# Forming the weight sums of the vs projection by chained adding transfers, and reordering its token tiles, splits and late additions

## The chip, the cores and the metric

The kernel runs on one core of one Trainium2 chip. The metric is the device time of one execution in microseconds (us); lower is better. A core has TensorE (PE; its weight loads are PEld), VectorE (DVE), ScalarE (ACT), GpSimd (POOL) and SyncE (SP), each with an instruction queue of its own that is worked off in order, and 16 DMA engines that SP, ACT and POOL start transfers on.

## The reference

One layer of a streaming encoder for 1024 tokens and 1024 channels, in float32:

```python
h = rmsnorm(x, norm_g)
q, k, v, za, u, vs, zs, gm = split(h @ w_in)
a = window_sink_attention(rope(q), rope(k), v, sinks)
a = (a * silu(za)) @ w_att_out
sgo = chunked_spatial_gating(gelu(u), gelu(vs), sg_w, sg_b, ln_g, ln_b)
sgo = (sgo * silu(zs)) @ w_sg_out
ga, gs = split(sigmoid(gm + b_merge))
x = x + (ga * a + gs * sgo) @ w_o
out = rmsnorm(x, final_g)
```

The change lies in the first stage: the norm of x and the projection `vs`, whose gelu goes through a layer norm (hence statistics per token) into the spatial gating.

## The kernel before, in words

Every 1024 x 1024 x 1024 product is done by seven products of halves instead of eight (Strassen's scheme in Winograd's form). For `vs` the four quarters of the weights are a11, a12, a21, a22, and the sums are s1 = a21 + a22, s2 = s1 + a11, s3 = a11 + a21, s4 = a12 + s2; the tokens' forms are called b11, b21, t1, b22, t2, t3, t4. Every float32 operand is split in two: ACT casts a high part to the matmul's type (`nc.scalar.copy`, L155 in `split`, L557 in `form_of`), and DVE subtracts it to leave a low part (L156 and L558). Each product is then made of three, high by high, high by low and low by high. A product for one token tile of 128 tokens is 12 matmuls of 128x512.

The weights come packed in 128 x 1024 pieces; a quarter is two of them (c = 0 and 1). The sums of weights are made by transfers: `add_on(dst, src)` is a GpSimd DMA that adds its source to the destination in SBUF (L531). a11 lies in the slot T_t3h, a12 in T_t3l, s1 (loaded as a21, then a22 added) in T_t4h; the slots are taken by token forms later. Before the change a12 first takes a11 from DRAM and then s1, which makes s4, and a11 takes s1, which makes s2: eight adding transfers of 512 KB.

The tokens come in eight tiles. `first_tile(t)`, t = 0 to 3, and `second_tile(t)`, t = 4 to 7, load x (three buffers `wr` for all loads, L487), square it on ACT (L536) for the norm, compute the scale on DVE and ACT (L133 to L145), scale by it and by the gain on DVE (L544), transpose on PE (L548) into a bank `ps_sc`, and form b11 and b21, or t1 and b22. The gain lies in two PSUM banks for tiles 0 and 1 (`g_in`, made by a product with ones); before the change ACT copies these to SBUF (`g_sb`, L709) for the later tiles. `second_tile` also keeps what t2, t3 and t4 are made of: it makes the raw sum (L580, and a second addition, L586), a copy f22 of the second half (L585), and two adding transfers for t3 and t4.

Around the tiles stand the products: `first_product(t)` (b11 by a11 into `accs[t]`, b21 by a12, whose sum is x11: ACT copies, L668, DVE adds, L669), `by_s1(t)` (t1 by s1, into `t5s[t]`, which ACT copies negated, L674) and `by_s4(t)` (b22 by s4, onto the same bank). Then three calls of `late_product` run t2 by s2, t3 by s3 and t4 by a22, each over c and t, with gelus (`gelu_of`, L761) and statistics (L757) of finished quarters and the splits of what comes next beside the matmuls. The products for `u` begin after that (L341, in `gemm_pair`).

`part_of_early` issues, at certain places, one step of a list of 76 GpSimd transfers that form weight sums of later projections in DRAM (L296); a step waits for the matmul at which it was issued. With an argument n it issues at every n-th call; the list must be empty after the attention, where each hook calls it with 2.

The order of instructions on each engine is not the order of the source. A scheduler lays it down ahead of time from a cost model and priorities by source order: an instruction that the model has ready earlier may be put ahead of one that stands before it in the source. `after(second, first)` adds an order between two instructions of one engine without a wait. A helper example:

```python
def gelu_of(t, half=0):
    two = xh[:, t : t + 2, half_of(half)]
    after(nc.scalar.activation(two, two, AF.Gelu), last_cast)
```

Other small pieces that the text speaks of: the mixing weights `mix_w` are loaded into the buffer `wT`, which the squares use as scratch until tile 7, and a part is cleared by DVE (L767, L768); the sinks are loaded into `sink_sb` and negated on DVE into `nsink_sb` (L831, L834), which the attention reads much later.

Of the kernel before, what the change touches and what calls it, by code (L numbers as in the profile page):

```python
# [24 lines left out]
F32 = mybir.dt.float32  # L25
# [27 lines left out]
def hybrid_tile(  # L53
# [474 lines left out]
    casts = []  # L528
# [22 lines left out]
    def form_of(name, t, src, minus=False):  # L551
        hi, lo = (v[:, :, tokens(t)] for v in hb[name])
        if minus:
            casts.append(nc.scalar.mul(hi, src, -1.0))
            nc.vector.scalar_tensor_tensor(lo, src, -1.0, hi.bitcast(F32), op0=ALU.mult, op1=ALU.subtract)
        else:
            casts.append(nc.scalar.copy(hi, src))  # L557
            nc.vector.tensor_sub(lo, src, hi.bitcast(F32))  # L558
# [15 lines left out]
    def second_tile(t):  # L574
        xt, r = scale_of(t)
        if t == 4:
            hb.update(new_b(("t1", "b22")))
            f22.append(slot("t4l", dt=F32))
        pt = turned_half(xt, r, 0)
        nc.vector.tensor_sub(raw_sum(t), raw_sum(t), pt[:])  # L580
        nc.scalar.mul(nf12[t - 4][:], pt[:], -1.0)
        form_of("t1", t, by_k(raw_sum(t)))
        pt = turned_half(xt, r, 1)
        form_of("b22", t, by_k(pt[:]))
        nc.scalar.copy(f22[0][:, t - 4, :], pt[:])  # L585
        nc.vector.tensor_add(raw_sum(t), raw_sum(t), pt[:])  # L586
        add_on(nf12[t - 4][:], f22[0][:, t - 4, :])
        add_on(raw_b21(t), raw_sum(t))
# [29 lines left out]
    def split_w(name, c, src=None):  # L618
        hi, lo = pair_of_w()
        split(hi[:], lo[:], flat(two_k(raws[name], c)) if src is None else src)  # L620
        keep_w(name, c, hi, lo)
# [41 lines left out]
    def first_product(t):  # L663
        accs[t] = bank("mm" if t < 2 else "tp")
        vs_product(accs[t], "b11", t, "a11", True)
        m2 = bank("o")
        vs_product(m2, "b21", t, "a12", True)
        nc.scalar.copy(x_place(0, 0, t), m2[:])  # L668
        nc.vector.tensor_add(x_place(0, 0, t), x_place(0, 0, t), accs[t][:])  # L669
# [23 lines left out]
    x_in[2] = load_x(2)  # L693
    load_part("s1", "t4h", 1, 0)
# [6 lines left out]
    for c in range(2):  # L701
        add_on(flat(two_k(raws["a12"], c)), w_vs(0, 0, c))
    for c in range(2):
        add_on(flat(two_k(raws["a12"], c)), flat(two_k(raws["s1"], c)))
    raws["s4"] = raws["a12"]
    first_tile(1, second)
    g_sb = xh[:, 6:8, HALF:D]
    for half in range(2):
        after(nc.scalar.copy(g_sb[:, half, :], g_in[half][:]), casts[-1])  # L709
# [5 lines left out]
    second_tile(4)  # L715
    s1_hl = slot("t2h"), slot("t2l")
    for c in range(2):
        hi, lo = (two_k(v, c) for v in s1_hl)
        split(hi, lo, two_k(raws["s1"], c))
        for k in range(2):  # L720
            vs_w["s1", 2 * c + k] = hi[:, k, :], lo[:, k, :]
    first_product(2)
    second_tile(5)
    for c in range(2):
        add_on(flat(two_k(raws["a11"], c)), flat(two_k(raws["s1"], c)))
    raws["s2"] = raws["a11"]
    first_product(3)
    for c in range(2):
        split_w("s4", c)
    second_tile(6)  # L730
    by_s1(0)
# [4 lines left out]
    second_tile(7)  # L736
    by_s4(0)
# [7 lines left out]
    last_cast = casts[-1]  # L745
    split_w("s2", 0)
    hb.update(new_b(("t2",)))
    for t in range(4):
        form_of("t2", t, by_k(raw_sum(t)), True)
    by_s4(2)  # L750
# [21 lines left out]
    def late_product(name, weight, done, aside):  # L772
        for c in range(2):
            for t in range(4):
                pace[0] = vs_product(accs[t], name, t, weight, False, cs=(c,))
                if t % 3:
                    part_of_early(1)
                elif c:
                    part_of_early()
# [46 lines left out]
    split_w("a22", 1, a22[1][:])  # L826
    begin_job()
# [6 lines left out]
    nc.vector.tensor_scalar_mul(nsink_sb[:], sink_sb[:], -1.0)  # L834
# [1027 lines left out]
```

## Time and profile before

| | |
|---|---|
| time, median of 3 runs | 940.05 us (937.19 to 940.18) |
| the profiled execution | 941.21 us, span 939.4 us |
| PE busy | 904.0 us, 96% of the span |
| DVE, ACT, POOL busy | 697.7, 528.3 and 142.9 us |
| DMA moved | 210.10 MB, mean 224 GB/s |

The profile is one execution. Its rows read: line of the source, engine, operation, output<-inputs, shape, count, busy time, and the idle time of the engine just before with what ended it. In a timeline the first two numbers are the start and the time in us. A row of windows gives busy time of each engine in one stretch, the clock granted to TensorE as a share of full speed, the busy share of the DMA engines and the GB/s that they moved.

### The profile page before, as it was taken

Reading aid. Unit: us, or ns where it says so; the run is one execution under the profiler, and the core shown is the slowest. Engines: PE = TensorE matmul, PEld = TensorE weight load, DVE = VectorE, ACT = ScalarE, POOL = GpSimd, SP = SyncE. Lnnn points to the kernel's source line nnn. Section 1 sums busy time; section 2 is a strip of 40 time slices with the busy share of each in tenths; the row PEclk is TensorE's granted clock in tenths of the full one; section 3 lists DMA queues with packets and bytes.
Section 4 is the critical chain, followed back from the end, with each engine's and each line's share of the span. In section 5 each row is a group of like instructions: output and inputs, shape, how many; then the busy total and the mean of one; then the engine's idle time right before and its main releaser. Section 6 shows DMA issues by size and latency. Waiting matters only on the chain.

```text
span 939.4 us, 13191 instructions
## 1 busy us (share of the span) xinstructions
PE 904.0 (96%) x4284; PEld 749.5 (80%) x4284; DVE 697.7 (74%) x1263; ACT 528.3 (56%) x1060; POOL 142.9 (15%) x206
## 2 busy tenths in 40 slices
PE   8779989999999989999999999999998999999996
PEld 6557868888888878888888888888886887888885
DVE  6566866666667667888888888746799489669986
ACT  6547442333445357766766766746575466458443
POOL 2121222221202001011111111101100010210012
PEclk9798999999999999999999999999999999999999
DMA  8894987886877765777877669789878754999623
GB/s 283 192 242 100 233 249 178 173 174 168 287 241 245 268 197 166 185 199 206 215 199 265 225 172 254 213 273 376 277 240 315 266 191 152 291 298 311 206 104 121
DMA packets 131615, 210.10 MB, mean 224 GB/s; under 512 B 12666, under 2 KB 61050, under 8 KB 131547
## 3 DMA queue, kind: packets, MB, share of 16 engines
q1 hardware_dynamic: 109800, 149.21, 47.6%
q0 software_dynamic: 21600, 59.78, 28.1%
q8 instruction: 34, 0.56, 0.3%
q14 instruction: 35, 0.28, 0.1%
q10 hardware_dynamic: 146, 0.27, 0.1%
HBM read 148.27 MB, written 86.11 MB: 250 GB/s over the span
## 4 chain that ended last, share of the span: by engine, by line
PE 80%; DVE 8%; DMA 7%; issue 2%; ACT 1%; SPq 0%; DVEq 0%; ACTq 0%
PE ps_mm L341 35%; PE ps_o L341 25%; PE ps_sc L1192 3%; DMA wr<-in_w_dram 3%; PE ps_tp L341 3%; PE ps_o L1277 2%; PE ps_sc L341 2%; PE ps_tp L1236 2%; PE ps_sc L650 1%; DVE wl L156 1%; DMA sink_sb<-in_sinks_dram 1%; PE ps_tp L650 1%; PE ps_tp L880 1%; PE ps_mm L650 1%; DMA wT<-in_sg_w_dram 1%
## 5 line engine op out<-in xcount | busy, mean ns | idle before, releaser
L155 ACT CAST wh<-s 128x1024 fp32r<-128x1024 f32 (+1 forms) x78 | 78.2, 1004 | 88.9 <-PE ps_mm L341 49.7
L156 DVE TENSOR_TENSOR wl<-wr,wh 128x1024 fp32r<-128x1024 f32 (+1 forms) x78 | 73.3, 942 | 45.5 <-ACT wh L155 43.8
L155 ACT CAST wh<-wr 128x1024 fp32r<-128x1024 f32 (+1 forms) x78 | 64.1, 824 | 63.0 <-PE ps_mm L341 30.4
L156 DVE TENSOR_TENSOR wl<-s,wh 128x1024 fp32r<-128x1024 f32 (+1 forms) x78 | 91.5, 1173 | 9.2 <-ACT wh L155 8.6
L341 PE MATMUL ps_o<-T_t1h,wh 128*128 128x512 f32 x148 | 58.8, 397 | 0.8 <-ACT wh L155 0.7
L341 PE MATMUL ps_o<-T_b22h,wh 128*128 128x512 f32 x148 | 58.2, 393 | 0.0
L341 PE MATMUL ps_mm<-T_b11h,wl 128*128 128x512 f32 x140 | 55.2, 394 | 2.9 <-DVE wl L156 2.9
L341 PE MATMUL ps_o<-T_b22l,wh 128*128 128x512 f32 x148 | 57.8, 391 | 0.0
L341 PE MATMUL ps_o<-T_b22h,wl 128*128 128x512 f32 x148 | 57.8, 390 | 0.0
L341 PE MATMUL ps_o<-T_t1h,wl 128*128 128x512 f32 x148 | 57.7, 390 | 0.0
L341 PE MATMUL ps_o<-T_t1l,wh 128*128 128x512 f32 x148 | 57.6, 389 | 0.0
L341 PE MATMUL ps_mm<-T_t3h,wh 128*128 128x512 f32 x140 | 55.1, 393 | 2.3 <-ACT x L366 2.3
L341 PE MATMUL ps_mm<-T_t4h,wh 128*128 128x512 f32 x140 | 55.4, 396 | 0.6 <-DVE x L376 0.6
L341 PE MATMUL ps_mm<-T_b11h,wh 128*128 128x512 f32 x140 | 55.4, 396 | 0.0
L341 PE MATMUL ps_mm<-T_t3l,wh 128*128 128x512 f32 x140 | 54.6, 390 | 0.6 <-DVE T_t3l L156 0.6
L341 PE MATMUL ps_mm<-T_t2l,wh 128*128 128x512 f32 x140 | 55.2, 394 | 0.0
L341 PE MATMUL ps_mm<-T_b11l,wh 128*128 128x512 f32 x140 | 55.1, 394 | 0.0
L341 PE MATMUL ps_mm<-T_t2h,wl 128*128 128x512 f32 x140 | 55.0, 393 | 0.0
L341 PE MATMUL ps_mm<-T_t2h,wh 128*128 128x512 f32 x140 | 55.0, 393 | 0.0
L341 PE MATMUL ps_mm<-T_t4h,wl 128*128 128x512 f32 x140 | 54.8, 392 | 0.0
L341 PE MATMUL ps_mm<-T_t4l,wh 128*128 128x512 f32 x140 | 54.8, 391 | 0.0
L1205 ACT ACTIVATE pr<-ps_sc,sm 128x192 f32<-128x192 f32 (+2 forms) x128 | 50.9, 410 | 6.7 <-DVE sm L1201 5.8
(382 smaller groups left out, 2413.8 us busy)
## 6 DMA issues: line engine op xcount, KB each, us to landing
wr<-in_w_dram SPq DMA_DIRECT2D x86, 256.0 KB
sums<-in_w_dram POOLq DMA_DIRECT2D x20, 512.0 KB, 8.5
s<-sums SPq DMA_DIRECT2D x20, 512.0 KB
q_hl<-qhl SPq DMA_DIRECT2D x16, 512.0 KB
q<-q_hl SPq DMA_DIRECT2D x64, 128.0 KB
y_dr<-x POOLq DMA_DIRECT2D x28, 256.0 KB, 6.4
wr<-in_w_dram SPq DMA_DIRECT2D x12, 512.0 KB
g<-in_w_dram POOLq DMA_DIRECT2D x12, 512.0 KB, 6.9
```

Of the source, the lines that this page charges most:

```text
L155: nc.scalar.copy(hi, src)
L156: return nc.vector.tensor_sub(lo, src, hi.bitcast(F32))
L341: nc.tensor.matmul(acc, lt, rt, start=fresh and k == 0 and n == 0, stop=k == 3 and n == 2, skip_group_check=True,)
L650: mm = nc.tensor.matmul(acc[:], lt, rt, start=fresh and k == 0 and n == 0, stop=k == 3 and n == 2, skip_group_check=True,)
L880: nc.tensor.matmul(pm[:, t * P : (t + 1) * P], xh[:, half * 4 + t, g * P : (g + 1) * P], bias[-1][1][:, g % 4, :], start=True, stop=True,)
L1192: nc.tensor.matmul(sc[:, i, k0:], q_of[:, c, i * P : (i + 1) * P], kt[:, f, k0:], start=f == 0, stop=f == 1,)
L1205: nc.scalar.activation(held_in[c, i], sc[:, i, lo:hi], AF.Exp, bias=nmax[:, c, i : i + 1], scale=-1.0, accum_out=sums[:, c, i : i + 1],)
L1236: nc.tensor.transpose(dst, pr[:, i, block * P : block * P + width], ident[:])
L1277: nc.tensor.matmul(po[:, cs], lt, rt, start=n == 0, stop=n == len(terms) - 1)
```

## The change

- The weight sums are chained: s1 is added to a11 (s2) and that to a12 (s4). Six adding transfers instead of eight, all issued early; the two of a11 had stood after `second_tile(5)`.
- The gain for tiles 2 to 7 is loaded by a broadcasting DMA on SP's queue, ahead of the loads for s1, in place of two ACT copies.
- `split_behind` is a split whose two instructions are ordered behind the last cast and the last low part of the token tiles so far. It is used for s1 (now ahead of `second_tile(4)` in the source), s4 and the first piece of s2.
- The second raw addition and the transfer behind it leave `second_tile` for `raw_t2(t)`, which reads f22 from SBUF; it is called for tile 4 after tile 6, and for the others after tile 7. The additions to x11 leave `first_product` for `to_x11(t)`, ordered behind the low parts of tile 7.
- `last_cast`, behind which the gelus are ordered, is now the last cast of t2.
- The steps of `part_of_early` in the three late products are 4, 4, 4 and one more between the second and the third, instead of 5, 5 and 5.
- The negation of the sinks is ordered behind the last low part (that of t4).

```diff
--- before.py
+++ after.py
@@ -525,7 +525,7 @@
         return x_place(1, 0, t)
 
     g_of = list(g_in)
-    casts = []
+    casts, lows = [], []
 
     def add_on(dst, src):
         nc.gpsimd.dma_start(dst, src, accum_op=ALU.add)
@@ -552,10 +552,16 @@
         hi, lo = (v[:, :, tokens(t)] for v in hb[name])
         if minus:
             casts.append(nc.scalar.mul(hi, src, -1.0))
-            nc.vector.scalar_tensor_tensor(lo, src, -1.0, hi.bitcast(F32), op0=ALU.mult, op1=ALU.subtract)
+            lows.append(
+                nc.vector.scalar_tensor_tensor(lo, src, -1.0, hi.bitcast(F32), op0=ALU.mult, op1=ALU.subtract)
+            )
         else:
             casts.append(nc.scalar.copy(hi, src))
-            nc.vector.tensor_sub(lo, src, hi.bitcast(F32))
+            lows.append(nc.vector.tensor_sub(lo, src, hi.bitcast(F32)))
+
+    def split_behind(hi, lo, src):
+        after(nc.scalar.copy(hi, src), casts[-1])
+        after(nc.vector.tensor_sub(lo, src, hi.bitcast(F32)), lows[-1])
 
     def first_tile(t, scale=None):
         xt, r = scale or scale_of(t)
@@ -583,8 +589,10 @@
         pt = turned_half(xt, r, 1)
         form_of("b22", t, by_k(pt[:]))
         nc.scalar.copy(f22[0][:, t - 4, :], pt[:])
-        nc.vector.tensor_add(raw_sum(t), raw_sum(t), pt[:])
         add_on(nf12[t - 4][:], f22[0][:, t - 4, :])
+
+    def raw_t2(t):
+        nc.vector.tensor_add(raw_sum(t), raw_sum(t), f22[0][:, t - 4, :])
         add_on(raw_b21(t), raw_sum(t))
 
     def w_vs(i, j, c):
@@ -615,9 +623,9 @@
         for k in range(2):
             vs_w[name, 2 * c + k] = hi[:, half_of(k)], lo[:, half_of(k)]
 
-    def split_w(name, c, src=None):
+    def split_w(name, c, src=None, behind=False):
         hi, lo = pair_of_w()
-        split(hi[:], lo[:], flat(two_k(raws[name], c)) if src is None else src)
+        (split_behind if behind else split)(hi[:], lo[:], flat(two_k(raws[name], c)) if src is None else src)
         keep_w(name, c, hi, lo)
 
     def split_vs(c):
@@ -666,7 +674,9 @@
         m2 = bank("o")
         vs_product(m2, "b21", t, "a12", True)
         nc.scalar.copy(x_place(0, 0, t), m2[:])
-        nc.vector.tensor_add(x_place(0, 0, t), x_place(0, 0, t), accs[t][:])
+
+    def to_x11(t):
+        after(nc.vector.tensor_add(x_place(0, 0, t), x_place(0, 0, t), accs[t][:]), lows[-1])
 
     def by_s1(t):
         t5s[t] = bank("o" if t < 2 else "sc")
@@ -691,6 +701,8 @@
     for c in (2, 3):
         load_vs(c)
     x_in[2] = load_x(2)
+    g_sb = xh[:, 6:8, HALF:D]
+    nc.sync.dma_start(g_sb, norm_g.partition_broadcast(P).rearrange("p (h n) -> p h n", h=2))
     load_part("s1", "t4h", 1, 0)
     for c in (2, 3):
         split_vs(c)
@@ -699,41 +711,40 @@
     for c in range(2):
         add_on(flat(two_k(raws["s1"], c)), w_vs(1, 1, c))
     for c in range(2):
-        add_on(flat(two_k(raws["a12"], c)), w_vs(0, 0, c))
+        add_on(flat(two_k(raws["a11"], c)), flat(two_k(raws["s1"], c)))
     for c in range(2):
-        add_on(flat(two_k(raws["a12"], c)), flat(two_k(raws["s1"], c)))
-    raws["s4"] = raws["a12"]
+        add_on(flat(two_k(raws["a12"], c)), flat(two_k(raws["a11"], c)))
+    raws["s2"], raws["s4"] = raws["a11"], raws["a12"]
     first_tile(1, second)
-    g_sb = xh[:, 6:8, HALF:D]
-    for half in range(2):
-        after(nc.scalar.copy(g_sb[:, half, :], g_in[half][:]), casts[-1])
     g_of[:] = [g_sb[:, half, :] for half in range(2)]
     first_tile(2)
     first_product(0)
     first_tile(3)
     first_product(1)
-    second_tile(4)
     s1_hl = slot("t2h"), slot("t2l")
     for c in range(2):
         hi, lo = (two_k(v, c) for v in s1_hl)
-        split(hi, lo, two_k(raws["s1"], c))
+        split_behind(hi, lo, two_k(raws["s1"], c))
         for k in range(2):
             vs_w["s1", 2 * c + k] = hi[:, k, :], lo[:, k, :]
+    second_tile(4)
     first_product(2)
     second_tile(5)
-    for c in range(2):
-        add_on(flat(two_k(raws["a11"], c)), flat(two_k(raws["s1"], c)))
-    raws["s2"] = raws["a11"]
     first_product(3)
     for c in range(2):
-        split_w("s4", c)
+        split_w("s4", c, behind=True)
     second_tile(6)
+    raw_t2(4)
     by_s1(0)
     by_s1(1)
     load_part("s3", "t4h", 1, 0)
     for c in range(2):
         add_on(flat(two_k(raws["s3"], c)), w_vs(0, 0, c))
     second_tile(7)
+    for t in range(4):
+        to_x11(t)
+    for t in (5, 6, 7):
+        raw_t2(t)
     by_s4(0)
     by_s4(1)
     a22 = []
@@ -742,11 +753,11 @@
         nc.sync.dma_start(a22[c][:], w_vs(1, 1, c))
     by_s1(2)
     by_s1(3)
-    last_cast = casts[-1]
-    split_w("s2", 0)
+    split_w("s2", 0, behind=True)
     hb.update(new_b(("t2",)))
     for t in range(4):
         form_of("t2", t, by_k(raw_sum(t)), True)
+    last_cast = casts[-1]
     by_s4(2)
     by_s4(3)
     split_w("s2", 1)
@@ -773,10 +784,8 @@
         for c in range(2):
             for t in range(4):
                 pace[0] = vs_product(accs[t], name, t, weight, False, cs=(c,))
-                if t % 3:
+                if t % 2:
                     part_of_early(1)
-                elif c:
-                    part_of_early()
                 if c:
                     done(t)
                 if aside:
@@ -824,6 +833,7 @@
         for n, part in enumerate((wh, wl)):
             nc.tensor.matmul(row_sums[half][:], ones[:], part[:, half_of(half)], start=n == 0, stop=n == 1)
     split_w("a22", 1, a22[1][:])
+    part_of_early(1)
     begin_job()
     late_product("t4", "a22", to_x21, [split_next, lambda: gelu_of(4, 1), lambda: gelu_of(6, 1)])
     of_head = sinks.rearrange("(c e r) -> e c r", e=2, r=2)
@@ -831,7 +841,7 @@
         nc.sync.dma_start(
             sink_sb[e * 64 : (e + 1) * 64].rearrange("p (c r) -> p c r", r=2), of_head[e].partition_broadcast(64)
         )
-    nc.vector.tensor_scalar_mul(nsink_sb[:], sink_sb[:], -1.0)
+    after(nc.vector.tensor_scalar_mul(nsink_sb[:], sink_sb[:], -1.0), lows[-1])
     nc.sync.dma_start(bm_sb[:], b_merge)
     nc.sync.dma_start(lg_sb[:], ln_g)
     nc.sync.dma_start(lb_sb[:], ln_b)
```

## The prediction

> **What bounds the kernel now.** I read the page first, then windows, then the waits of PE, then the timelines of ACT and DVE around its long waits.
>
> ```profile
> span 939.4 us, 13191 instructions
> PE 904.0 (96%) x4284; PEld 749.5 (80%) x4284; DVE 697.7 (74%) x1263; ACT 528.3 (56%) x1060; POOL 142.9 (15%) x206
> ```
> ```profile
> 2.00:15.00 13.00, 12.50 (x34) 7.66 (x35) 7.58 (x18) 9.53 (x18) 2.16 (x2) 1.00 0.99 388
> 36.00:42.00 6.00, 6.00 (x27) 4.87 (x26) 3.43 (x11) 2.45 (x7) 0.00 (x0) 0.78 1.01 201
> 28.00:40.00 12.00, 8.54 (x27) 6.36 (x27) 6.15 (x13) 6.19 (x11) 3.46 (x4) 0.57 1.05 236
> 66.00:78.00 12.00, 9.22 (x29) 7.21 (x30) 6.77 (x13) 6.27 (x9) 3.45 (x4) 0.58 0.78 155
> 0.00:118.30 118.30, 101.30 (x412) 78.16 (x413) 79.19 (x154) 67.66 (x112) 27.15 (x40) 0.91 0.82 211
> 118.30:939.40 821.10, 802.69 (x3873) 671.32 (x3871) 618.47 (x1110) 460.62 (x948) 115.78 (x166) 0.99 0.75 225
> ```
>
> Columns of a window: its length, busy time of PE, PEld, DVE, ACT and POOL, granted clock, DMA share, GB/s. PE is the bound: 904.0 of 939.4 us. Idle time is uneven: 17.0 of 118.3 us before 118.3 us, at clock 0.91; 18.4 of 821.1 after it, at 0.99. The first U product starts at 118.30, so the first stretch is exactly the stage of the vs products, which the change rewrites:
>
> ```profile
> 118.30 0.39 PE L341 MATMUL ps_mm<-T_b11h,wh 128*128 128x512 f32 x1
> ```
>
> Its PE waits (total, times, longest):
>
> ```profile
> PE ps_tp L650 <- ACT T_b11h L557: 5.0, 1, 5.0
> PE ps_sc L548 <- DVE wr L544: 4.3, 1, 4.3
> PE ps_o L650 <- ACT xh L674: 2.1, 2, 1.8
> PE ps_tp L650 <- DVE T_b11l L558: 1.7, 1, 1.7
> PE ps_sc L650 <- ACT x L581: 1.2, 1, 1.2
> ```
>
> None of these is a slow instruction. Each is an engine standing, in its own order, before an instruction whose transfer has not landed, with ready work behind it:
>
> ```profile
> 28.15 1.04 ACT L155 CAST T_t2h<-T_t4h 128x1024 fp32r<-128x1024 f32 x1 [6.56 <-DMA T_t4h<-in_w_dram]
> 29.10 0.58 ACT L557 CAST T_b11h<-ps_sc 128x512 fp32r<-128x512 f32 x1
> 51.15 1.06 ACT L536 ACTIVATE wT<-wr 128x1024 f32<-128x1024 f32 x1 [2.08 <-DMA wr<-in_x_dram]
> 52.21 0.58 ACT L674 ACTIVATE xh<-ps_o 128x512 f32<-128x512 f32 x1
> ```
> ```profile
> 31.55 0.20 DVE L834 TENSOR_SCALAR nsink_sb<-sink_sb 128x8 f32<-128x8 f32 x1 [9.77 <-DMA sink_sb<-in_sinks_dram]
> 64.83 0.48 DVE L768 MEMSET wT<- 64x512 f32 x1 [5.15 <-DMA wT<-in_sg_w_dram]
> ```
>
> ACT holds the split of the weight sum s1 (reading T_t4h) ahead of tile 2's cast T_b11h and stands 6.56 us for the adding transfer: PE loses 5.0. DVE holds the sinks' negation, 9.77 us: tile 2's T_b11l is late and PE loses 1.7 more. The loss of 1.8 comes from x tile 6, for which ACT waits ahead of L674. The 4.3 us loss is DVE at the memset of the mixing weights. After each of the two long stops the clock is near half: 0.57 over 28 to 40 us, 0.58 over 66 to 78.
>
> **Part by part.** Sums are made against the profiled execution, 941.21 us (span 939.4 plus 1.8); the median shown, 940.05, is 1.2 below it.
>
> *s1's split behind tile 3's casts and low parts.* ACT's instruction after tile 2's transposes becomes T_b11h, and DVE's T_b11l, if the nsink step is moved too (it is: it stands behind the last low part, t4's). PE's 5.0 and 1.7 go: -6.7. The split now queues in front of token tile 4, and s1 is first read by by_s1(0). Its two casts of 1.04 and two low parts of about 1.23 lie beside the 24 matmuls of first_product(3), where PE is busy. ACT and DVE must then keep up:
>
> ```profile
> L156 DVE TENSOR_TENSOR wl<-T_t3h,wh 128x1024 fp32r<-128x1024 f32 x3 | 3.7, 1226 | 2.2 <-ACT wh L155 2.2
> ```
> ```profile
> 22.20:60.00 37.80, 29.12 (x127) 22.59 (x126) 23.70 (x52) 21.40 (x40) 7.85 (x10) 0.86 0.93 215
> ```
>
> In these 37.8 us, 25.6 after the gain summed below, ACT has 21.4 us of work and DVE 23.7, of which five additions of 0.68 move away. Both fit, ACT at 84%; this is why I count no gain beyond the stops named.
>
> *The half-speed stretch after it.* In 28 to 40 us PE was busy 8.54 us at 0.57; at full clock the same work takes 4.9: -3.7. It goes because its cause, the long stop, goes. The Trainium skill, "TensorE: Matmul & The Clock Gate", Part 1, has the clock halve after an idle window of about 3.4 us and return after about 3.4 us of sustained work. By that length the stretch is worth only an estimated 1.7 and the whole sum is 2.0 smaller; the row shows a longer one, and the row is used.
>
> *Tile 6's load.* In SP's queue it stands behind s3's load, which needs T_t4h free:
>
> ```profile
> SPq L604 <- DMA T_t3h<-T_t4h: 19.3, 2, 16.8
> ```
> ```profile
> 44.77 0.33 SPq L604 DMA_DIRECT2D T_t4h<-in_w_dram  x1
> 45.20 0.80 SPq L487 DMA_DIRECT2D wr<-in_x_dram  x1
> ```
>
> T_t4h is read last by the add that makes s2 (T_t3h), which was the eighth and last add in the queue and becomes the fourth of six. By the rates below it lands near 30.5 (16.4 + 4 x 2.6 + 2.7, and 1 for handing over). So x6 is issued near 31 us, not 45.2, and the 1.8 goes: -1.8. If the two loads change places the result is the same, since x6's buffer is free when tile 3 is transposed.
>
> *One add less per half, in a chain.* Before, a12 took a11 from DRAM and then s1; now s1 goes to a11 (s2) and s2 goes to a12 (s4). Adds fall from eight to six, but s4 hangs from three in a row instead of two.
>
> ```profile
> T_t3l<-in_w_dram POOLq DMA_DIRECT2D x2, 512.0 KB, 7.8
> T_t4h<-in_w_dram POOLq DMA_DIRECT2D x2, 512.0 KB, 12.6
> T_t3l<-T_t4h POOLq DMA_DIRECT2D x2, 512.0 KB, 9.7
> T_t3h<-T_t4h POOLq DMA_DIRECT2D x2, 512.0 KB, 11.7
> ```
> ```profile
> 14.31 1.04 POOL L531 DMA_DIRECT2D T_t3l<-in_w_dram  x1 [5.76 <-DVE st L140]
> 16.55 2.05 POOL L531 DMA_DIRECT2D T_t4h<-in_w_dram  x2
> 31.20 0.85 POOL L531 DMA_DIRECT2D T_t3l<-T_t4h  x1 [0.77 <-DMA T_t4h<-in_w_dram]
> ```
>
> The last number of the first four rows is the median time to landing. With the DMA full, plain loads moved 388 GB/s (2 to 15 us) and adds alone 201 (36 to 42): 1.35 and 2.6 us for 512 KB. The a12 adds at 14.31 stood ahead of s1's at 16.55; now s1's are first. Loads end near 16.4 (15 plus 1.35 for the gain's broadcast). Six adds and x4 and x5 are 15.7 + 2.7 = 18.4 us of transfers; with 2 us for handing over between links, an estimate by these rates puts the last half of s4 at about 37, where before its add was issued at 31.20 and landed about 9.7 later, near 41. s4 is first read at
>
> ```profile
> 52.84 0.74 PE L650 MATMUL ps_o<-wh,T_b22h 128*128 128x512 f32 x2 [1.81 <-ACT xh L674]
> ```
>
> which becomes 52.8 - 12.2 = 40.6; less 2.3 for cast and low part, it is wanted by 38.3. I take 0, with one or two us to spare; this is the thinnest cover of all, and the rivals price it.
>
> *Gain by broadcast instead of two ACT copies.*
> ```profile
> 18.48 0.61 ACT L709 COPY xh<-ps_tp 128x512 f32<-128x512 f32 x1
> 20.25 1.42 DVE L544 SCALAR_TENSOR_TENSOR wr<-wr,st,xh 128x512 f32<-128x512 f32 x2
> 24.13 0.61 PE L650 MATMUL ps_o<-s,T_b21l 128*128 128x512 f32 x2
> ```
>
> The two copies removed (0.61 each, from 18.48) ran while PE was busy until 24.7: 0. The added load stands in SP's queue ahead of s1's parts and x3. Like a load it costs 1.35 us of DMA; at double price, 2.7, x3 lands near 18, and its tile is scaled only after tile 2's. Tile 2's scaling, at 20.25, finds the gain landed near 13: 0 directly; its delay is in the 37 above.
>
> *Adds to x11 and raw sums, gelus, later.* Eight DVE additions like these move behind tile 7's low parts, and four statistics behind t2's:
>
> ```profile
> L586 DVE TENSOR_TENSOR xh<-xh,ps_sc 128x512 f32<-128x512 f32 x4 | 2.7, 684 | 0.1
> L757 DVE BATCH_NORM_STATS2 bn<-xh 128x6 f32<-128x512 f32 x14 | 8.9, 680 | 3.5 <-ACT xh L761 3.5
> ```
> ```profile
> 72.00:84.70 12.70, 12.70 (x48) 10.25 (x48) 6.50 (x11) 9.57 (x15) 1.71 (x2) 0.84 0.38 84
> 84.70:118.30 33.60, 33.60 (x149) 27.78 (x148) 29.04 (x48) 17.81 (x23) 9.11 (x14) 1.00 0.78 203
> ```
>
> At most 8 x 0.68 = 5.5 us enter the first of these stretches and 4 x 0.68 = 2.7 leave it: DVE 6.5 + 2.8 = 9.3 of 12.7. The second gets 2.7: 31.8 of 33.6. Both fit, the second tightly: 0, at most +2. The later adds of raw_b21 land after the last of these additions, and keep_t5, which overwrites their source, may stand on ACT for it: 0 to +2, covered by the t2 product, a third of that second stretch.
>
> *Early sums.* 13 steps instead of 15 are issued in this stage, and two more fall to the attention, whose 70 hooks at every second one take 35. No wait of PE there names them: 0, between -0.5 and +1.
>
> *Left as it is.* The memset at 64.83 has no new order, so I keep its 4.3, the 1.2 behind it and its slow clock (9.22 x 0.42 = 3.9).
>
> Sum: -6.7 - 3.7 - 1.8 = -12.2. 941.2 - 12.2 = 929.0 for the profiled execution; less 1.2, about 927 to 928 for the median. After 118.3 PE idles 2% only, so the gain is carried to the end. I forecast 927.
>
> **Rivals.**
>
> *The memset's stop goes too.* x6 and x7 load ten us earlier, so sg_w, issued behind tile 7's square, does too; if PE then still has by_s4 and by_s1 products in hand, the 4.3 + 1.2 + 3.9 = 9.4 also go: 927.8 - 9.4 = 918. For it: DVE is lightened. Against: its place in DVE's order still precedes tile 7's scaling.
>
> *s4 a few us late.* If its second half lands at about 42 to 43, ACT stands before the cast and by_s4 waits some 4 to 5 us: 932 to 933, and with a half-speed stretch after it 936.
>
> *Slower: the chain of three sets the pace.* Say each link takes what the slowest kind took, 12.6: issued near 15.5, s4 would land at 15.5 + 37.8 = 53.3, be split at 55.6, and PE, at 40.6, would stand 15.0 us and then lose 3.7 to the clock: 18.7 against 12.2, so 946. It decides from a landing near 46.8 (46.8 + 2.3 - 40.6 + 3.7 = 12.2). For it: landings of 9.7 to 12.6. Against: those had four adds in flight, and there are only two at a time in a chain. The Trainium skill, "DMA: Bandwidth & Descriptors", Anatomy of one DMA, gives a fixed 2.0 us plus bytes over 436 GB/s. By it a link is an estimated 3.2 us, and the rival is out of reach; the rows here, slower at every add, do not agree, and I keep the rival.
>
> *It does not carry.* The U weights and their sums, loaded behind a full DMA, could hold the U pairs at the old time: about 940. Against: they are issued by buffers that PE's progress frees, not by time.
>
> **How the numbers follow.** Forecast 0.45; memset also gone 0.20; s4 a few us late 0.20; not carried 0.06; slower 0.09. A measurement of this kernel can tell about 0.3%, 2.8 us. The first three are faster: 0.85; same 0.06; slower 0.09. The range runs from 916 (memset gone, with two us more) to 937 (s4 late, with slow clock), leaving out the last two cases and a little below.
>
> **What would show it.** Right: no ACT wait on T_t4h ahead of T_b11h, PE without a gap at 24.7, clock 1.00 over 28 to 40, the first L341 matmul near 106. The waits list should have no nsink_sb and no long L604 on T_t3h. Wrong: a PE wait at by_s4 with ACT's cast of T_t3l held by a transfer (the chain), a PE wait behind a new DVE or ACT stop of over 3 us, or an early first L341 matmul with new idle time between 118 and 160.

## The result and the profile after

The changed kernel takes 930.88 us (median of 4 runs, 930.13 to 932.78) against 939.87 us before on the same chip (4 runs, 937.19 to 940.18): a ratio of 0.9914 [0.989, 0.9937], 9.0 us less. The profiled execution takes 930.13 us against the 941.21 of the one before.

From the page of the kernel after, the span and the engines' busy time:

```profile
span 928.4 us, 13190 instructions
PE 898.3 (97%) x4284; PEld 746.8 (80%) x4284; DVE 697.0 (75%) x1263; ACT 526.9 (57%) x1058; POOL 141.5 (15%) x204
```

The same windows of it (length, busy PE, PEld, DVE, ACT, POOL, granted clock, DMA share, GB/s), the first two cut at its first U product:

```profile
0.00:107.93 107.93, 95.91 (x412) 75.00 (x413) 78.25 (x150) 66.40 (x110) 24.29 (x36) 0.98 0.81 222
107.93:928.40 820.47, 802.35 (x3873) 671.77 (x3871) 618.76 (x1114) 460.51 (x948) 117.18 (x168) 0.99 0.76 226
28.00:40.00 12.00, 8.93 (x43) 6.81 (x41) 7.62 (x17) 8.22 (x17) 2.06 (x3) 1.00 0.95 230
60.00:66.00 6.00, 5.92 (x23) 4.44 (x23) 4.80 (x9) 3.03 (x5) 0.86 (x1) 0.72 1.05 234
66.00:78.00 12.00, 12.00 (x55) 9.94 (x54) 6.58 (x9) 9.46 (x15) 1.31 (x2) 1.00 0.21 37
0.00:60.00 60.00, 48.06 (x207) 35.85 (x208) 39.08 (x88) 36.98 (x69) 14.52 (x22) 1.00 0.92 263
60.00:80.00 20.00, 19.92 (x84) 16.06 (x84) 13.38 (x20) 14.49 (x23) 2.48 (x3) 0.91 0.48 109
```

The whole gain lies in the stage of the vs products: it ends at 107.93 instead of 118.30, 10.4 us earlier, and the rest takes 820.5 instead of 821.1. Of the 10.4, 5.4 are PE work done at a better clock (busy 95.91 instead of 101.30) and 5.0 are idle time (12.0 instead of 17.0).

PE's waits of the stage (total, times, longest):

```profile
PE ps_sc L548 <- issue: 5.2, 2, 4.6
PE ps_sc L548 <- ACT T_t4l L591: 2.9, 1, 2.9
PE ps_sc L497 <- DVE T_b22l L493: 1.9, 1, 1.9
PE ps_sc L548 <- DVE wr L544: 1.6, 1, 1.6
```

The timelines of ACT, DVE, PE and SP's queue around the places that the prediction names (start, us, what it is, idle time before it and its releaser):

```profile
21.75 0.59 ACT L559 CAST T_b11h<-ps_sc 128x512 fp32r<-128x512 f32 x1 [0.55 <-PE ps_sc L548]
29.32 1.06 ACT L563 CAST T_t2h<-T_t4h 128x1024 fp32r<-128x1024 f32 x1
35.99 1.06 ACT L536 ACTIVATE wT<-wr 128x1024 f32<-128x1024 f32 x1 [3.70 <-DMA wr<-in_x_dram]
46.75 1.06 ACT L563 CAST wh<-T_t3l 128x1024 fp32r<-128x1024 f32 x1 [0.45 <-DMA T_t3l<-T_t3h]
48.20 1.05 ACT L536 ACTIVATE wT<-wr 128x1024 f32<-128x1024 f32 x1
57.36 0.48 DVE L779 MEMSET wT<- 64x512 f32 x1 [4.79 <-DMA wT<-in_sg_w_dram]
59.00 1.42 DVE L544 SCALAR_TENSOR_TENSOR wr<-wr,st,xh 128x512 f32<-128x512 f32 x2
49.69 0.62 PE L658 MATMUL ps_o<-wh,T_b22h 128*128 128x512 f32 x2
59.85 1.80 PE L548 MATMUL ps_sc<-ident,wr 128*128 128x128 f32 x8 [4.64 <-issue]
28.88 1.11 SPq L487 DMA_DIRECT2D wr<-in_x_dram  x1
37.50 1.46 SPq L612 DMA_DIRECT2D T_t4h<-in_w_dram  x2
39.08 0.42 SPq L487 DMA_DIRECT2D wr<-in_x_dram  x1
49.36 0.33 SPq L778 DMA_DIRECT2D wT<-in_sg_w_dram  x1
```

ACT casts tile 2 at 21.75 and only then s1 (29.32), without standing for it; the stop at the negation of the sinks is gone, and the wait of SP's queue ahead of s3's load is 4.8 us at the longest (16.8 before). What is new: ACT stands 3.70 us for x tile 5 (PE loses the 2.9 behind T_t4l). What has stayed: DVE stands 4.79 us at the memset of the mixing weights, for the load sg_w, with tile 7's scaling (59.00) behind it, and PE stands 4.64 for that. PE's "issue" of 59.85 is this stop: what PE does next are the transposes of tile 7, just behind the scaling.

The three rows of SP's queue at 37.50, 39.08 and 49.36 are the ones to hold on to. They are s3's load, tile 7's x (x7), and sg_w. In the kernel before, the queue and ACT show of the last two, and of tile 7's square between them:

```profile
47.06 0.33 SPq L487 DMA_DIRECT2D wr<-in_x_dram  x1
54.06 1.06 ACT L536 ACTIVATE wT<-wr 128x1024 f32<-128x1024 f32 x1 [1.18 <-DMA wr<-in_x_dram]
55.43 0.87 SPq L767 DMA_DIRECT2D wT<-in_sg_w_dram  x1
```

The chain of work that ended last in that kernel, followed back in its trace, runs through the same places (start, us, what; three of its pieces):

```profile
47.06 6.91 DMA wr<-in_x_dram
55.43 9.25 DMA wT<-in_sg_w_dram
66.80 0.76 DVE wr L544
```

So there is a chain in the kernel before. s3's load waits for the last add that reads T_t4h; x7 stands behind it in the queue; tile 7's square waits for x7; sg_w goes into the square's scratch buffer and so waits for the square; the memset waits for sg_w; tile 7's scaling stands behind the memset. The memset is at 64.83 before and at 57.36 after. The experiments ask whether the stage ends by this chain or by the stops that the prediction added up.

### The profile page after: what moved, and what is told of

Read it like the earlier page. It is cut to its first block, busy times and chain, and to the rows that moved or that the text cites. A ratio compares the mean times of both kernels' runs of the same rounds, so it can differ in the third digit from the quotient of the medians.

```text
span 928.4 us, 13190 instructions
## 1 busy us (share of the span) xinstructions
PE 898.3 (97%) x4284; PEld 746.8 (80%) x4284; DVE 697.0 (75%) x1263; ACT 526.9 (57%) x1058; POOL 141.5 (15%) x204
## 4 chain that ended last, share of the span: by engine, by line
PE 74%; DMA 9%; DVE 9%; issue 4%; ACT 1%; POOL 1%; SPq 1%; DVEq 0%; POOLq 0%; ACTq 0%
PE ps_mm L341 35%; PE ps_o L341 25%; PE ps_sc L1202 3%; DMA wr<-in_w_dram 3%; DMA T_t4h<-in_w_dram 3%; PE ps_tp L341 3%; PE ps_o L1287 2%; PE ps_sc L341 2%; PE ps_tp L1246 2%; DMA T_t3h<-T_t4h 2%; DVE wl L156 2%; PE ps_tp L890 2%; DVE bq L185 1%; DMA sums<-in_w_dram 1%; DVE xh L868 1%
## 5 line engine op out<-in xcount | busy, mean ns | idle before, releaser
L155 ACT CAST wh<-s 128x1024 fp32r<-128x1024 f32 (+1 forms) x78 | 78.1, 1004 | 86.0 <-PE ps_mm L341 46.8
L341 PE MATMUL ps_o<-T_t1h,wh 128*128 128x512 f32 x148 | 58.8, 397 | 0.8 <-ACT wh L155 0.7
L341 PE MATMUL ps_o<-T_b22h,wh 128*128 128x512 f32 x148 | 58.2, 394 | 0.0
L341 PE MATMUL ps_o<-T_b22l,wh 128*128 128x512 f32 x148 | 57.9, 391 | 0.0
L341 PE MATMUL ps_o<-T_b22h,wl 128*128 128x512 f32 x148 | 57.8, 390 | 0.0
L341 PE MATMUL ps_o<-T_t1h,wl 128*128 128x512 f32 x148 | 57.7, 390 | 0.0
L341 PE MATMUL ps_o<-T_t1l,wh 128*128 128x512 f32 x148 | 57.6, 389 | 0.0
L341 PE MATMUL ps_mm<-T_b11h,wl 128*128 128x512 f32 x140 | 54.8, 392 | 2.9 <-DVE wl L156 2.9
L341 PE MATMUL ps_mm<-T_t3h,wh 128*128 128x512 f32 x140 | 55.5, 397 | 2.0 <-ACT x L366 2.0
L341 PE MATMUL ps_mm<-T_t4h,wh 128*128 128x512 f32 x140 | 55.2, 394 | 0.8 <-DVE x L376 0.7
L341 PE MATMUL ps_mm<-T_t3l,wh 128*128 128x512 f32 x140 | 55.3, 395 | 0.6 <-DVE T_t3l L156 0.6
L341 PE MATMUL ps_mm<-T_t3h,wl 128*128 128x512 f32 x140 | 55.4, 395 | 0.0
L341 PE MATMUL ps_mm<-T_b11h,wh 128*128 128x512 f32 x140 | 55.2, 395 | 0.0
L341 PE MATMUL ps_mm<-T_b11l,wh 128*128 128x512 f32 x140 | 54.8, 392 | 0.0
L341 PE MATMUL ps_mm<-T_t4h,wl 128*128 128x512 f32 x140 | 54.7, 391 | 0.0
L341 PE MATMUL ps_mm<-T_t2l,wh 128*128 128x512 f32 x140 | 54.6, 390 | 0.0
L341 PE MATMUL ps_mm<-T_t2h,wl 128*128 128x512 f32 x140 | 54.5, 390 | 0.0
L341 PE MATMUL ps_mm<-T_t4l,wh 128*128 128x512 f32 x140 | 54.5, 390 | 0.0
```

The lines of the kernel that those rows point to most:

```text
L341: nc.tensor.matmul(acc, lt, rt, start=fresh and k == 0 and n == 0, stop=k == 3 and n == 2, skip_group_check=True,)
```

## The experiments

The expectations call the account on record theory A: the two early stops of ACT and DVE and the slow clock behind them are the gain. Each run stands beside runs of the kernel before on the same chip.

**Orders alone, the sinks' negation alone, the chain of adds alone, and the change without the chain.** The first leaves the eight adds, the gain's copies and the additions as before and takes over only the orders:

```diff
-    nc.vector.tensor_scalar_mul(nsink_sb[:], sink_sb[:], -1.0)
+    after(nc.vector.tensor_scalar_mul(nsink_sb[:], sink_sb[:], -1.0), lows[-1])
...
-    second_tile(4)
     s1_hl = slot("t2h"), slot("t2l")
...
-        split(hi, lo, two_k(raws["s1"], c))
+        split_behind(hi, lo, two_k(raws["s1"], c))
...
+    second_tile(4)
...
-        split_w("s4", c)
+        split_w("s4", c, behind=True)
...
-    split_w("s2", 0)
+    split_w("s2", 0, behind=True)
```

> The kernel before with only the orders of the change: s1, s4 and the first piece of s2 split behind the token tiles' casts and low parts, s1's split ahead of tile 4, the sinks' negation behind the last low part. Adds, gain copies, gelus, x11 and raw sums and early steps stay as before. Theory A (the two stops of ACT and DVE and the slow clock after them are the gain): PE runs on without the 5.0 and 1.7 us waits, 8 to 11 us faster than before, near 930 to 932. Rival B (fewer and earlier adding transfers are the gain): s1's sum lands as late as before, by_s1 waits for it instead, 0 to 3 us faster.

Measured: 938.38 us, ratio 0.9987 [0.997, 1.0005]. Its timelines of SP's queue, ACT and DVE; PE's longest wait; two windows:

```profile
46.85 0.80 SPq L610 DMA_DIRECT2D T_t4h<-in_w_dram  x2
47.77 0.36 SPq L487 DMA_DIRECT2D wr<-in_x_dram  x1
53.43 1.06 ACT L536 ACTIVATE wT<-wr 128x1024 f32<-128x1024 f32 x1 [4.61 <-DMA wr<-in_x_dram]
64.69 0.48 DVE L774 MEMSET wT<- 64x512 f32 x1 [6.92 <-DMA wT<-in_sg_w_dram]
```
```profile
PE ps_sc L548 <- DVE wr L544: 12.0, 2, 8.7
```
```profile
0.00:60.00 60.00, 50.40 (x208) 37.77 (x208) 39.57 (x87) 37.72 (x71) 15.51 (x23) 0.97 0.89 246
60.00:80.00 20.00, 11.94 (x41) 9.58 (x42) 9.59 (x15) 8.58 (x13) 2.57 (x3) 0.66 0.77 169
```

The same two windows of the kernel before:

```profile
0.00:60.00 60.00, 48.78 (x194) 35.63 (x195) 38.40 (x86) 37.08 (x69) 13.73 (x22) 0.91 0.91 240
60.00:80.00 20.00, 14.22 (x52) 10.84 (x51) 9.20 (x16) 8.14 (x13) 4.31 (x5) 0.74 0.79 188
```

The orders do what they say: by 60 us PE has done 208 matmuls instead of 194, as many as the changed kernel (207), and the clock is 0.97 instead of 0.91. Then they lose it all: x7 is issued at 47.77, close to the 47.06 before, the memset is at 64.69 as before, and PE stands 12.0 us in two waits for a scaling: 3.3 for tile 4's, until 35.15, and 8.7 for tile 7's behind the memset, until 66.88 (4.3 before). Between 60 and 80 us PE does 41 matmuls against 52 before and 84 after. The early stops had been cover for a later wait, and theory A falls.

```diff
-    nc.vector.tensor_scalar_mul(nsink_sb[:], sink_sb[:], -1.0)
+    after(nc.vector.tensor_scalar_mul(nsink_sb[:], sink_sb[:], -1.0), lows[-1])
```

> The kernel before with only the sinks' negation ordered behind the last low part. Theory A: ACT's stop at s1's split remains (5.0 us of PE), only the 1.7 us behind it and a little of the slow clock go: 1 to 3 us faster. Rival (DVE's stop of 9.8 us is the larger cause): 5 us faster or more.

Measured: 941.23 us, ratio 1.0006 [0.9982, 1.0029]: nothing, where theory A had 1 to 3 us.

```diff
     for c in range(2):
-        add_on(flat(two_k(raws["a12"], c)), w_vs(0, 0, c))
+        add_on(flat(two_k(raws["a11"], c)), flat(two_k(raws["s1"], c)))
     for c in range(2):
-        add_on(flat(two_k(raws["a12"], c)), flat(two_k(raws["s1"], c)))
-    raws["s4"] = raws["a12"]
+        add_on(flat(two_k(raws["a12"], c)), flat(two_k(raws["a11"], c)))
+    raws["s2"], raws["s4"] = raws["a11"], raws["a12"]
...
-    for c in range(2):
-        add_on(flat(two_k(raws["a11"], c)), flat(two_k(raws["s1"], c)))
-    raws["s2"] = raws["a11"]
```

> The kernel before with only the adds of the change: s1 first, then s1 to a11, then that to a12, six instead of eight, all early. Theory A: s1's adds are no longer behind those of a12, so ACT's stop shrinks from 6.6 to some 2 to 4 us, DVE's stop at the sinks stays: 1 to 4 us faster. Rival B: 7 us faster or more, as the whole change is.

Measured: 929.22 us, ratio 0.9886 [0.9857, 0.9916]: all of the gain, from the part that the prediction put at 0, without any of the orders. Its timelines of SP's queue and DVE, and a window:

```profile
34.59 1.05 SPq L604 DMA_DIRECT2D T_t4h<-in_w_dram  x2
35.75 2.82 SPq L487 DMA_DIRECT2D wr<-in_x_dram  x2
58.13 0.48 DVE L765 MEMSET wT<- 64x512 f32 x1 [0.16 <-DMA wT<-in_sg_w_dram]
```
```profile
60.00:80.00 20.00, 18.82 (x86) 15.21 (x87) 13.85 (x21) 15.52 (x25) 4.14 (x5) 1.00 0.53 116
```

The add that makes s2, the last reader of T_t4h, is no longer at the end of the queue of adds: s3's load goes at 34.59 (44.77 before) and x6 and x7 right behind it (both in the row of 35.75, x7 at 38.24). And s1's adds are the first on the queue, so that ACT, with the old order, does not stand before s1's split (its cast is at 22.21, where before it was at 28.15). PE still has early stops (2.5 us for T_b11l, 4.6 behind ACT's L674), and by 60 us it has done 197 matmuls, 3 more than before. What has gone is the late stop: the memset waits 0.16 us, no wait of PE for a scaling is left, and between 60 and 80 us PE does 86 matmuls instead of 52, at a clock of 1.00 instead of 0.74.

The last of the four is the changed kernel with the eight adds of before:

```diff
-        add_on(flat(two_k(raws["a11"], c)), flat(two_k(raws["s1"], c)))
+        add_on(flat(two_k(raws["a12"], c)), w_vs(0, 0, c))
...
-        add_on(flat(two_k(raws["a12"], c)), flat(two_k(raws["a11"], c)))
-    raws["s2"], raws["s4"] = raws["a11"], raws["a12"]
+        add_on(flat(two_k(raws["a12"], c)), flat(two_k(raws["s1"], c)))
+    raws["s4"] = raws["a12"]
...
     second_tile(5)
+    for c in range(2):
+        add_on(flat(two_k(raws["a11"], c)), flat(two_k(raws["s1"], c)))
+    raws["s2"] = raws["a11"]
```

> The changed kernel with the eight adds of before at their old places, all else changed. Theory A: the splits stand behind the token tiles, so a later s1 is covered: within 2 us of the changed kernel, 929 to 933. Rival B: the gain goes, 936 to 940. The slower rival of the prediction (the chain sets the pace) would make this one faster than the changed kernel by 3 us or more.

Measured: 940.07 us, ratio 0.9998 [0.9981, 1.0015]: all of the gain lost, with every order in place. Its DVE:

```profile
65.61 0.48 DVE L782 MEMSET wT<- 64x512 f32 x1 [6.18 <-DMA wT<-in_sg_w_dram]
```

By their times the three runs that test rival B, that fewer and earlier adds are the gain, go its way.

**x7 ahead of s3's load.** What the chain of adds changes is either the adds themselves or the place at which they free T_t4h. Theory C: two gates in series, (1) the early stops and (2) x7 behind s3's load in SP's queue; each alone is worth little, because it hides behind the other, and both together all of it, with the eight adds too. The edit puts s3's load and adds behind x7's load, with and without the orders:

```diff
-    load_part("s3", "t4h", 1, 0)
+    second_tile(7)
+    load_part("s3", "t4h", 1, 0, x_loads[-1])
     for c in range(2):
         add_on(flat(two_k(raws["s3"], c)), w_vs(0, 0, c))
-    second_tile(7)
```

> The orders-only kernel (eight adds as before) with one more order: on SP's queue the load of s3 and its adds stand behind the x load of tile 7. Theory C (new: the stage ends some 70 us after tile 7's x load is issued, and that load stands behind s3's, which waits for the last add that reads s1): x7 is issued near 38 instead of 47.8 us, 7 to 10 us faster than the kernel before. Rival D (fewer adds help by less traffic of DMA, wherever the x load stands): no more than 2 us from the 938 of the orders alone.

> The kernel before with only this: the load of s3 and its adds stand behind tile 7's x load on SP's queue. Theory C: x6 can go at about 40 us, x7 at 44 to 45 (their buffers, with the early stops of ACT and DVE still there), so 2 to 4 us faster; together with the orders-only run and the run with both, a gain that only both bring together shows two stops in a row, each hiding the other. Rival D: within 1 us of before.

Measured: with the orders 928.97 us, ratio 0.9888 [0.9873, 0.9904]; without them 939.82 us, ratio 1.0001 [0.999, 1.0011]. SP's queue, DVE and two windows of the kernel with both:

```profile
36.86 0.33 SPq L487 DMA_DIRECT2D wr<-in_x_dram  x1
55.53 0.48 DVE L777 MEMSET wT<- 64x512 f32 x1 [2.45 <-DMA wT<-in_sg_w_dram]
```
```profile
0.00:60.00 60.00, 49.64 (x216) 36.92 (x216) 43.20 (x94) 38.87 (x74) 16.33 (x24) 1.00 0.94 261
60.00:80.00 20.00, 19.92 (x81) 16.38 (x82) 13.34 (x19) 15.65 (x24) 3.19 (x4) 0.91 0.72 157
```

And SP's queue and DVE of the kernel with x7 first alone, and the longest of the queue's waits:

```profile
40.00 4.53 SPq L487 DMA_DIRECT2D wr<-in_x_dram  x2
63.24 0.48 DVE L771 MEMSET wT<- 64x512 f32 x1 [4.98 <-DMA wT<-in_sg_w_dram]
```
```profile
SPq L487 <- DVE wr L545: 26.6, 4, 14.1
```

So both together bring all of it with the eight adds too, and rival D falls. Alone, x7 first brings x7 forward only to 44.20 (the second load in the row of 40.00), as expected, because now the queue waits up to 14.1 us for the buffers of x6 and x7, which the tiles ahead free late while the early stops are there; the 2 to 4 us that were expected of it did not come (the stage ends 1.2 us earlier, the time is the same). The orders alone leave x7 behind s3's load. Seven kernels side by side (us; all have the memset ahead of tile 7's scaling):

| kernel | x7 issued | tile 7 squared | memset | first L341 | from memset to L341 | ratio |
|---|---|---|---|---|---|---|
| before | 47.06 | 54.06 | 64.83 | 118.30 | 53.5 | 1 |
| orders alone | 47.77 | 53.43 | 64.69 | 117.15 | 52.5 | 0.9987 |
| x7 first alone | 44.20 | 51.38 | 63.24 | 117.10 | 53.9 | 1.0001 |
| after, eight adds | 48.83 | 55.52 | 65.61 | 116.54 | 50.9 | 0.9998 |
| orders and x7 first | 36.86 | 47.59 | 55.53 | 107.56 | 52.0 | 0.9888 |
| chain of adds alone | 38.24 | 49.95 | 58.13 | 109.69 | 51.6 | 0.9886 |
| after | 39.08 | 48.20 | 57.36 | 107.93 | 50.6 | 0.9914 |

The stage ends 50.6 to 53.9 us behind the memset, in kernels whose memset lies anywhere from 55.5 to 65.6; the kernel with the sinks' negation alone fits too (64.74 and 118.42). The reason is that PE has hardly a gap behind that point: of its 12.0 us of idle time in the changed kernel 11.9 lie before 60 us, and of the 17.0 in the kernel before all lie before 80 us. What did not move that point was worth nothing, however much PE time it freed ahead of it. In the chain of adds alone the point is a mark of time and not a stop, since PE waits for no scaling there.

Does the changed kernel gain by x7 first as well?

> The changed kernel with s3's load and adds behind tile 7's x load. Theory C: x7 is issued near 36 instead of 39.1 us, but ACT squares it at 48 without waiting for it, so the load is no longer what ends last: within 1.5 us of the changed kernel. If the load still sets the end here, 3 us faster.

Measured: 929.77 us, ratio 0.9901 [0.988, 0.9922], level with the change. x7 goes at 34.6, but the memset still waits 4.73 us for sg_w, at 58.45, and the stage ends 51.5 us behind it, at 109.99.

**The memset behind tile 7, in the changed kernel.** If the memset is the point, then ordering it behind the last low part must pay:

```diff
-    nc.vector.memset(mix_w[64:128, :, 0:64], 0.0)
+    after(nc.vector.memset(mix_w[64:128, :, 0:64], 0.0), lows[-1])
```

> The changed kernel with the clearing of the mixing weights on DVE ordered behind the last low part so far (that of t2). The stop of DVE at 52.6 to 57.4 us goes, and with it PE's 4.6 us wait and the slow clock of 60 to 64 us (1.7 us): 5 to 6 us faster than the changed kernel, 925. If the token tiles are late for another reason (tile 7's scaling held by ACT), under 2 us.

Measured: 925.59 us (920.68 to 927.11), ratio 0.9844 [0.9812, 0.9877] against 0.9914 [0.989, 0.9937] of the change. The first L341 is at 103.56; the memset is at 68.55 and waits for nothing. That is 5.3 us by the medians, which come from two chips, and 0.7% by the ratios. The stop of 4.64 and the slow clock behind it (0.72 over 60 to 66 us, 6 x 0.28 = 1.7) come to 6.3, so most of what such a stop was reckoned at by its length and its slow clock was won.

**The deferred additions.** The change moved the raw additions, the additions to x11 and the gelus to later places. Undone in the changed kernel, with the memset left free:

```diff
+        nc.vector.tensor_add(raw_sum(t), raw_sum(t), pt[:])
         add_on(nf12[t - 4][:], f22[0][:, t - 4, :])
-
-    def raw_t2(t):
-        nc.vector.tensor_add(raw_sum(t), raw_sum(t), f22[0][:, t - 4, :])
...
-    def to_x11(t):
-        after(nc.vector.tensor_add(x_place(0, 0, t), x_place(0, 0, t), accs[t][:]), lows[-1])
+        nc.vector.tensor_add(x_place(0, 0, t), x_place(0, 0, t), accs[t][:])
...
+    last_cast = casts[-1]
     split_w("s2", 0, behind=True)
...
-    last_cast = casts[-1]
```

> The changed kernel with the raw additions back in the token tiles, the additions to x11 back in the first products without an order, and the gelus behind tile 7's casts again. By the prediction's zero for this part: within 2 us of the changed kernel, 929 to 933. If the deferral keeps DVE free where the tiles need it, 3 us slower or more.

Measured: 925.68 us, ratio 0.9852 [0.9829, 0.9875]: without the deferral the changed kernel is 5.2 us faster by the medians and 0.6% by the ratios, which neither side of the expectation had. Its DVE:

```profile
54.99 0.75 DVE L544 SCALAR_TENSOR_TENSOR wr<-wr,st,xh 128x512 f32<-128x512 f32 x1
57.32 0.48 DVE L770 MEMSET wT<- 64x512 f32 x1 [0.39 <-DMA wT<-in_sg_w_dram]
```

The memset is at the same time as after (57.36), but tile 7's scaling is now ahead of it and not behind. So in the changed kernel the memset comes ahead of the scaling with the three deferrals and behind it without them. That the scheduler put it into the place that the additions left, because its model expected sg_w earlier than it lands, is the likely reason; no run shows it. Nor is the deferral all of it: the kernel before, the orders alone and the orders with x7 first defer nothing and have the memset ahead of the scaling too.

**Eight adds with both orders and the memset behind** is the kernel with orders and x7 first plus the memset's order: no chain, no broadcast of the gain, no deferral, the old steps of early sums.

> Eight adds as in the kernel before, with the orders of the change, tile 7's x load ahead of s3's, and the clearing of the mixing weights behind t2's low parts: none of the chain, the broadcast gain, the later additions. Theory C: the chain of adds is one of two ways to bring tile 7's load forward, so this is level with the changed kernel with the memset moved, 924 to 928. If fewer adds are worth something of their own, 3 us slower than that or more.

Measured: 925.52 us (924.55 to 925.70), ratio 0.9851 [0.9827, 0.9875], level with the changed kernel with the memset's order. So fewer adds, the broadcast and the deferral, taken together, bring nothing that the two orders don't.

**The sinks' loads behind a22's.** In the changed kernel the new stop for x tile 5 follows a stretch in which the DMA engines do almost nothing. The sinks' loads, 2 KB each in small packets (1150 packets under 512 B over 14 to 40 us, 640 without these loads), stand in front of x tile 5 on SP's queue (18.43 and 22.45). Moved behind a22's loads, with the memset's order kept:

```diff
-        nc.sync.dma_start(a22[c][:], w_vs(1, 1, c))
+        a22_load = nc.sync.dma_start(a22[c][:], w_vs(1, 1, c))
...
+        after(of_sinks, a22_load)
```

> The changed kernel with the clearing of the mixing weights behind t2's low parts, as in the run before it, and the sinks' two small loads ordered on SP's queue behind the loads of a22. If the sinks' small packets are what leaves the DMA nearly idle from 25 to 29 us and lets x tile 5 land 14 us after its issue, the DMA gap goes, tile 5 is squared at about 32 instead of 37 us, PE's 4.1 us wait at its transposes goes: 3 to 4 us faster than the memset run, 922. If the gap has another cause, within 1.5 us of 925.6.

Measured: 923.16 us (921.28 to 925.39), ratio 0.983 [0.9801, 0.9859]. The window of 25 to 29 us, first after, then this kernel:

```profile
25.00:29.00 4.00, 4.00 (x23) 3.38 (x22) 1.16 (x4) 2.30 (x6) 0.85 (x1) 1.00 0.17 44
```
```profile
25.00:29.00 4.00, 4.00 (x23) 3.34 (x23) 2.63 (x8) 3.83 (x8) 0.85 (x1) 1.00 1.11 273
```

The gap is filled (273 instead of 44 GB/s) and ACT no longer stands for x tile 5. In time the interval overlaps that of the memset's order alone (0.9812 to 0.9877), so these 2.4 us by the medians of two chips are not separated from nothing.

> The run above with s3's load and adds also behind tile 7's x load. Theory C says that in the changed kernel x7's load is no longer last: within 1.5 us of the run above. If earlier stops had hidden it, 2 us faster or more.

Measured: 923.93 us (922.79 to 929.92), ratio 0.985 [0.9813, 0.9888]: x7 first adds nothing to it. These two are the fastest versions, 7 to 8 us below the change by the medians.

## Why the prediction was right, and where its reasons were not

The total was near: 929.0 forecast for the profiled execution, 930.13 measured; 927 for the median, 930.88 measured, a gain of 9.0 where about 13 was forecast. The reason was not right, and the terms do not stand as they were summed; that they came near the total is luck.

- **The two stops, −6.7.** Both went, as foreseen: the cast at 21.75, 0.2 us of wait left behind T_b11h. But alone they are worth nothing (ratio 0.9987). The step that failed is adding PE's waits up: these ended ahead of a later wait whose end is set by other work, and with the orders alone that wait grew from 4.3 to 8.7 us, with a new one of 3.3 at tile 4's scaling.
- **The half-speed stretch, −3.7.** The clock of 28 to 40 us is 1.00 (0.86 with the orders alone), and the same holds: with the orders alone PE had done 131 matmuls by 40 us instead of 107 and waited longer before 66.88. What the clock saved in the end, 5.4 us of busy PE time, needed both gates open: the orders alone saved 1.8 (99.50 instead of 101.30), x7 first alone nothing (101.71).
- **Tile 6's load, −1.8.** The observation was right and the reading too small. x6 went at 28.88, forecast near 31, though not as reckoned: T_t4h came free near 37.4 and not 30.5, and x6 went first because it stands ahead of s3's load in the queue now, the case that the prediction named. But s3's load also held x7, and x7 holds the square, sg_w, the memset and tile 7's scaling: this term was one of the two gates of the stage. With the orders x7 first is 9.6 us (117.15 to 107.56 in L341), without them 1.2 in the stage and nothing in time.
- **The chain of adds, 0.** Its lateness was under-sized and harmless, and its use was missed. s4's second half landed at about 46.7 and not at 37: from issue to landing the three links took 7.8, 11.2 and 7.7 us by their medians over 8 to 40 us:

```profile
T_t4h<-in_w_dram POOLq DMA_DIRECT2D x2, 512.0 KB, 7.8
T_t3h<-T_t4h POOLq DMA_DIRECT2D x2, 512.0 KB, 11.2
T_t3l<-T_t3h POOLq DMA_DIRECT2D x2, 512.0 KB, 7.7
```

  The forecast counted the queue's rate and about 1 us of handing over for each; the rows of landing times, which it kept for the rival, were the better price: 46.7 lies nearer to the rival's 53.3 than to 37. It is also where the slower rival was to decide (46.8). That rival did not come, since PE reached by_s4 at 49.69, without a wait there, and not at 40.6: at that point the gain was 3.2 us only, and most of the rest was won after it. What the chain alone brings (0.9886) is read from its trace: T_t4h is free ten us earlier, and s1's adds are first. These two effects of it were not tried one without the other; that they are the two gates rests on the runs with the orders and with x7 first.
- **Deferral, 0 to +2.** It cost 5.2 us, by a way not foreseen: not through work that came late, but with the memset ahead of tile 7's scaling.
- **Left as it is: the memset.** Right in result: the stop stayed (4.64 of PE against 4.3), and the slow clock behind it shrank to the 0.72 over 60 to 66 us. The rival in which it goes (918) did not come in the changed kernel; with the memset ordered behind t2's low parts the time is 925.6, about 5 us less, where it was priced at 9.4. In the chain of adds alone the stop did go.
- **Not foreseen:** the stop of 2.9 for x tile 5.
- **It carries.** The rest took 820.5 against 821.1, as argued.

So the total was near without its steps being the cause. Had the change had the orders without the chain, the same working would have forecast about −10, and the measured ratio is 0.9987.

Not tried alone: the broadcast and the steps of early sums; the memset's order on the kernel before or with the orders; and the sinks' loads without the memset's order. So how much of the second gate is x7 itself, and how much the memset ahead of the scaling, stays open. An estimate: with eight adds, both orders and the memset behind, tile 7's scaling starts 5.8 us after its square (47.30 to 53.05), with the orders alone 12.5 us after it (53.43 to 65.88). At 5.8 us it would start near 59 with the orders alone, where x7 first brought it to 56.72; so the memset's order might have opened much of the second gate by itself. That the stretch ahead of x tile 5 is held up by the small packets of the sinks is inferred from the filled gap, not shown by itself.

## What to carry to other kernels

Waits of one engine in one stage can't simply be added up: an early stop may be cover for a later one, and what counts is the last stop behind which the engine runs without a gap. Look for it backward from the last stop, through the queue that issues its load and what stands ahead of it there, and test parts in pairs, because two gates in series can each measure as zero. When instructions are moved later, look at how the rest of the order has changed, above all where an instruction that waits for a transfer now stands.

## What the runs showed of the hardware

- An adding transfer of 512 KB in a chain took 7.7 to 11.2 us from issue to landing, with the DMA share at 0.95 over 28 to 40 us; two of them were in flight at a time. That is three to four times the 2.6 us that its bytes take at the 201 GB/s of adds alone, which the kernel before shows over 36 to 42 us.
- Two sinks' loads of 2 KB each stood ahead of a 512 KB load that was issued at 22.45 and for which ACT waited until 35.99, 13.5 us, while over 25 to 29 us the DMA share was 0.17. With them moved away the share over the same 4 us was 1.11. That the small loads hold up the large one is inferred from this.
- After the stop of 4.64 us the clock was 0.72 over 60 to 66 us, which is 3.4 us at half speed (6 x 0.28 / 0.5); taken over each us it was 0.50 from 61 to 63 and 1.00 again from 64, 4.1 us after PE went on at 59.85. In the kernel before it was 0.57 over the twelve from 28 to 40: PE went on at 29.73, stood again for 1.7 us, went on without a gap from 33.53, and the clock was back at about 38.6. The Trainium skill, "TensorE: Matmul & The Clock Gate", Part 1, has the clock come back after at least one busy window of about 3.4 us of sustained work. Both stops fit it: 4.1 and about 5 us of work almost without a gap.
